# Two layer norms of a convolution mixer moved among other products, and one convolution tile moved from GpSimd to VectorE

## The chip, the cores and the metric

The kernel runs on one core of a Trainium2 chip. The metric is the device time of one execution in microseconds (us). The engines are TensorE (PE: matrix products; PEld: the loads of their weights), VectorE (DVE), ScalarE (ACT), GpSimd (POOL) and SyncE (SP), which issues the transfers. Each engine runs its own instructions strictly in order and waits for the others at semaphores.

## What is computed

Two layers on a sequence of 1024 tokens of width 1024. Layer 0 is a convolution mixer with a layer norm inside, layer 1 a pooling mixer:

```python
def _conv_mixer(h, w_in, dw, db, ln_g, ln_b, w_out):
    a, b, g = jnp.split(h @ w_in, 3, axis=-1)
    y = a * jax.nn.sigmoid(b)
    y = lax.conv_general_dilated(y, dw[:, None, :], ...)  + db     # 31 taps, each channel by itself
    y = jax.nn.silu(_layernorm(y, ln_g, ln_b)) * jax.nn.silu(g)
    return y @ w_out

def _pool_mixer(h, w_in, w_grp, scale, w_out):
    v, g = jnp.split(h @ w_in, 2, axis=-1)
    ...                                                            # window means, products by group
    return (y * jax.nn.silu(g)) @ w_out

for i in range(DEPTH):                                             # per layer
    h = _rms(x, norm_g[i]) * (1.0 + sc) + sh                       # sc, sh, gt from c @ w_mod
    x = x + gt * o
```

## The kernel before

Channels lie on the 128 partitions (8 tiles `ct`), tokens along the row, in two halves `h` of 512. Each float32 operand is split into a high and a low part (`load_split`: ScalarE writes the high part, VectorE or GpSimd the low one), and a product is three matmuls (`mm3`); a whole 1024-deep product (`gemm`) is 24 matmuls into one PSUM bank. The second half's part of layer 0 is worked off beneath the first half's layer 1, since its convolutions run on engines that are free there.

- **Convolutions** (`conv`, `conv_taps`). VectorE does a tile in two PSUM banks of the pool `cv` (tile name `cv`, L482). The tiles in `POOL_CT[h]` go another way: ScalarE multiplies by a tap into `pr` (L469), of which there are two buffers, and GpSimd adds it to `z` (L470). So ScalarE can be at most two taps ahead of GpSimd, and whatever stands behind a tap in ScalarE's order waits too.
- **Gates** (`gate_g`): the products `psg` with weights `wg`; the result goes to DRAM as `sgd` and comes back in `gate_norm`. `CORD` is the order of the tiles: 0, 2, 1, 3, 4, 6, 5, 7. The tiles in `FILL` (4, 6, 5, 7) have their second half done later, beneath another norm.
- **Layer norm** (`layernorm`): TensorE sums over channels (`mr`), ScalarE copies the row, TensorE spreads the mean (`mu`), VectorE subtracts it (L538), ScalarE squares (`sqz`, two buffers), TensorE sums the squares (`vpz`, 128x1 matmuls, L275), then ScalarE, GpSimd (power, `vrz`, L241), ScalarE (`dgz`) and TensorE (`rbz`) make the factor. `gate_norm` then applies factor, silu and gate to each tile and splits it into `y1`, which the output products `pso` need.
- **Layer 1** (`layer1_group`): products `psv` and `psq`, window means on VectorE (`s`), group products `psy`; `layer1_out` does the output products `psf`, four weights at a time first (`wp0` to `wp3`), then one by one.

The order on each engine comes from a scheduler that works by priority from the order of the code; `behind(...)` holds instructions after others, `priority(-LATER)` brings them forward.

Of the kernel before, what the change touches and what calls it, by code (L numbers as in the profile page):

```python
# [12 lines left out]
ALU = mybir.AluOpType  # L13
# [4 lines left out]
KT = 8  # L18
# [3 lines left out]
EPS = 1e-6  # L22
PAD = 8
FIRST = 4
POOL_CT = ((1, 3, 5), (1, 3, 5, 6, 7))
PAIRS = ((0, 2), (1, 3), (4, 6), (5, 7))
CORD = [ct for p in PAIRS for ct in p]
FILL = (4, 6, 5, 7)
# [6 lines left out]
HOLD = (4, 2, 3, 4)  # L35
GAPS = (2, 3, 1, 3)
LAST = 2
SUBS = (2, 4)
MID_OUT = 6
TAIL = 8  # L40
NA = HW - TAIL
# [15 lines left out]
def hybrid_kernel(ctx, tc, xT, vecs, wm, wk, cv_first, cv_w, cv_wo, pl_w, pl_grp, pl_wo, out):  # L57
    nc = tc.nc
# [7 lines left out]
    LATER = 1 << 20  # L66
# [3 lines left out]
    @contextmanager  # L70
    def priority(shift):
        base = tc.cur_priority
        tc.cur_priority = base + shift
        yield
        tc.cur_priority = base

    def step(n=1):
        for _ in range(n):
            if pending and next(pending[0], None) is None:
                pending.pop(0)  # L80

    def unit(tag, name, dt=F32, cols=1024):

        width = WIDTH.get(tag[0], 1024)
        return S.tile([P, width], dt, tag=tag, name=name, bufs=RINGS.get(tag, 1))[:, :cols]
# [4 lines left out]
    def raw(name):  # L90
        return unit("raw", name)

    def bank(tag, name):
        return PS.tile([P, HW], F32, tag=tag, name=name, bufs={"mm": 5, "ax": 1, "cv": 2}[tag])

    def mmps(name):
        return bank("mm", name)
# [4 lines left out]
    def hs(h):  # L102
        return slice(h * HW, (h + 1) * HW)

    def bl(j):
        return slice(j * P, (j + 1) * P)
# [8 lines left out]
    def pair(region, i, name):  # L115
        return unit(f"{region}{i}", name + "h", F32R), unit(f"{region}{i + 1}", name + "l", F32R)
# [48 lines left out]
    def hi_part(hi, src, add=None):  # L165
        if add is None:
            return nc.scalar.copy(hi, src)  # L167
        return nc.scalar.activation(hi, src, AF.Identity, bias=add)
# [15 lines left out]
    @contextmanager  # L184
    def behind(instructions):
        with ExitStack() as stack:
            for i in instructions:
                stack.enter_context(tc.issue_after(i.ins))
            yield
# [5 lines left out]
    def load_split(src, name, slots=None, load=nc.sync.dma_start, eng=nc.vector):  # L195
        r = raw(name)
        load(out=r, in_=src)
        u = pair(*slots, name) if slots else (unit("w", name + "h", F32R), unit("w", name + "l", F32R))
        hi_part(u[0], r)
        lo_part(*u, r, eng=eng)  # L200
        return u
# [24 lines left out]
    power_done, spread_done = [None], [None]  # L226
# [41 lines left out]
    def square_sums(xs, name, vp):  # L268


        def add(i):
            sq = half("sq", f"sq{name}{i}")
            nc.scalar.activation(sq, xs[i], AF.Square)  # L273
            for j in range(4):
                last = nc.tensor.matmul(  # L275
                    vp[:, j : j + 1], sq[:, bl(j)], ones[:, 0:1], start=i + j == 0, stop=i == KT - 1,
                    skip_group_check=True,
                )
            return last

        return (None, vp), add
# [102 lines left out]
    with priority(-LATER):  # L384
        x_done, rb = norm_x(0)
# [59 lines left out]
    def conv(h, ct, taps=None, count=None):  # L445

        with priority(LATER * (1 + h)):
            for _ in islice(taps or conv_taps(h, ct), count):
                pass

    def conv_taps(h, ct):
# [9 lines left out]
        order = [MID, MID - 1] + [k for k in range(TAPS) if k not in (MID, MID - 1)]  # L461
        if ct in POOL_CT[h]:
            for k in order:
# [38 lines left out]

    sgd = [[DR.tile([P, 1024], F32, name=f"sgd{h}{j}") for j in range(4)] for h in range(2)]

    def gate_g(ct, halves, after=(), start=KT // 2):
        wg = load_split(cv_w[2 * KT + ct], f"wg{ct}{halves[0]}")
        for h in halves:
            ps = mmps(f"psg{ct}{h}")
            gemm(ps, wg, hT[h], after, start)
            s = half("sg", f"sgw{ct}{h}")  # L510
            nc.scalar.activation(s, ps, AF.Silu)
            i = CORD.index(ct)
            nc.sync.dma_start(out=sgd[h][i // 2][:, hs(i % 2)], in_=s)

    for i, ct in enumerate(CORD[:6]):
        gate_g(ct, (0,) if ct in FILL else (0, 1))
        step(MODS[1][i])

    sums_done = [None, None]

    def layernorm(h, fill=None, after=None):
        z = [zs[h][ct] for ct in CORD]
        sums = mmps(f"mr{h}")
        row = S.tile([P, HW], F32, tag="row", name=f"mrow{h}", bufs=1)
        mu = axps(f"mu{h}")
        with priority(-LATER):
            for i, ct in enumerate(ZORD[h]):
                g = slice(32 * (i % 4), 32 * (i % 4) + 32)
                nc.tensor.matmul(sums[g, :], onesd[:, :32], zs[h][ct], start=i < 4, stop=i >= 4)
            nc.scalar.copy(row, sums)  # L530
            last = nc.tensor.matmul(mu, selm, row, start=True, stop=True)
        sums_done[h] = last
        if fill is not None:
            fill(GAPS[0], last)
        total, add = square_sums(z, f"z{h}", mmps(f"vpz{h}"))
        for i in range(KT):
            with behind([after[k] for k in range(2) if i >= SUBS[k]] if after else []):
                sub = nc.vector.tensor_tensor(out=z[i], in0=z[i], in1=mu, op=ALU.subtract)  # L538
            with priority(-LATER):
                add(i)  # L540
        if fill is not None:
            fill(GAPS[1], sub)
        return z, *rstd_rows(total, f"z{h}", fill)
# [79 lines left out]
        with behind([ins]):  # L623
            conv(1, 0, early_taps, count)

    z, rb, rb_done = layernorm(0, fill)
    gate_g(CORD[6], (0,), [rb_done], HOLD[0])
    gate_g(CORD[7], (0,), [rb_done], 0)
    y1, done = gate_norm(0, z, rb)
    with behind(done[1:]):  # L630
        conv(1, 0, early_taps)
        for ct in (1, 3):
            conv(1, ct)
        taps = conv_taps(1, 2)
        conv(1, 2, taps, EARLY)
    x1, total = out_half(0, y1, ws, done)
# [8 lines left out]
    h2_0, h2_started, h2_done, rb_done = h2_half(0, x1, total, "Q", 0)  # L645
# [12 lines left out]
    y2, mixed, rest = [[], []], [None, None], []  # L658
# [138 lines left out]
    for g in range(4):  # L797
        group = layer1_group(g, 0, h2_0, early, group if g else None)
        if g == 0:
            with behind([h2_done]):  # L800
                conv(1, 2, taps)
                for ct in range(4, KT):
                    conv(1, ct)
        if g:
            ahead += [load_split(pl_wo[m], f"wp{m}0", ("E", 2 * m)) for m in ((0,), (1,), (2, 3))[g - 1]]
    layer1_out(0, range(MID_OUT - 1), ahead, group)
    with priority(-LATER):
        z, rb, rb_done = layernorm(1, None, mixed)
    with behind(spread_done):
        for finish, m, ps in rest:  # L810
            finish(m, ps)
# [4 lines left out]
    x1, total = out_half(1, y1, ws, done)  # L816
    h2_1, _, _, rb_done = h2_half(1, x1, total, "Y", 2)
# [58 lines left out]
```

## Time and profile before

| | us |
|---|---|
| runs shown (3): median, lowest, highest | 798.62, 798.11, 800.89 |
| profiled execution: its own time | 799.68 |
| span of its instructions | 797.9 |
| busy: PE, DVE, POOL, ACT | 742.0, 555.5, 457.3, 400.9 |

The profiled execution took 799.68 us, of which 797.9 us are the span between its first and its last instruction. Times in the trace count from the start of that span. A busy TensorE is not one at its peak, since its clock has two levels, 1.2 and 2.4 GHz; the granted clock of a stretch is given as a share of the higher one.

### The profile page before, as it was taken

The page shows a single profiled execution, that of the slowest core. Times are in us where ns is not written, and L with a number is a line of the kernel's source. Part 1 is how long each engine was busy: PE and PEld are TensorE (multiplying, and loading weights), DVE is VectorE, ACT ScalarE, POOL GpSimd, SP SyncE. Part 2 cuts the span into 40 slices and gives each one's busy share as a digit, 9 for nine tenths or more (in the row PEclk, how much of TensorE's full clock was granted, in tenths as well). Part 3 has the DMA queues.
Part 4 walks back from the last instruction along what each step waited for, and adds up shares of the span by engine and source line. Part 5 has one row for each costly group of instructions (what it writes and reads, how often), then busy time and mean ns, then how long its engine had stood idle before and what let it go on. Part 6 is the DMA issues. An engine that isn't in the chain of part 4 may idle for free.

```text
span 797.9 us, 9925 instructions
## 1 busy us (share of the span) xinstructions
PE 742.0 (93%) x3564; PEld 590.1 (74%) x3564; DVE 555.5 (70%) x721; ACT 400.9 (50%) x590; POOL 457.3 (57%) x386
## 2 busy tenths in 40 slices
PE   3899999999999968989999879998899889999998
PEld 1777787777776647658877657886788668888998
DVE  6998997928894270899969999973295562566521
ACT  4446466565667677643786665431323432433210
POOL 2001989999988999850999995180112521443322
PEclk7799999999999985999999989999699989999999
DMA  9880013424147550344541124547123630233232
GB/s 328 323 307 25 0 63 123 159 106 153 67 151 300 215 172 1 107 125 152 187 156 53 53 93 131 185 137 257 40 93 119 199 117 1 93 106 132 80 108 81
DMA packets 36481, 105.68 MB, mean 132 GB/s; under 512 B 4048, under 2 KB 6224, under 8 KB 36432
## 3 DMA queue, kind: packets, MB, share of 16 engines
q1 hardware_dynamic: 36432, 105.05, 38.0%
q8 instruction: 28, 0.46, 0.2%
q14 instruction: 21, 0.17, 0.1%
HBM read 92.45 MB, written 12.58 MB: 132 GB/s over the span
## 4 chain that ended last, share of the span: by engine, by line
PE 32%; POOL 30%; DVE 14%; issue 11%; ACT 8%; DMA 3%; SPq 0%; POOLq 0%; ACTq 0%; DVEq 0%
POOL z L470 27%; DVE cv L482 3%; PE psv L206 2%; PE psq L206 2%; PE psq L204 2%; PE psq L205 2%; PE psv L204 2%; PE psv L205 2%; PE psf L204 2%; PE psf L205 2%; PE psf L206 2%; ACT pr L469 2%; PE pso L204 2%; PE pso L205 2%; PE pso L206 2%
## 5 line engine op out<-in xcount | busy, mean ns | idle before, releaser
L470 POOL TENSOR_TENSOR z<-z,pr 128x512 f32<-128x512 f32 (+8 forms) x240 | 348.4, 1452 | 68.0 <-ACT z L466 40.5
L469 ACT ACTIVATE pr<-y,VT 128x512 f32<-128x512 f32 (+8 forms) x240 | 171.0, 719 | 117.6 <-POOL z L470 111.4
L482 DVE SCALAR_TENSOR_TENSOR cv<-y,VT,cv 128x512 f32<-128x512 f32 (+12 forms) x232 | 157.7, 740 | 0.2
L766 DVE SCALAR_TENSOR_TENSOR xf<-psf,gt,xf 128x260 f32<-128x260 f32 (+1 forms) x24 | 13.3, 570 | 38.2 <-PE psf L206 32.1
L241 POOL TENSOR_TENSOR vrx<-vex,mhalf 128x4 f32<-128x4 f32 x2 | 2.0, 1025 | 56.5 <-ACT vex L239 56.5
L560 DVE TENSOR_TENSOR z<-z,rbz 128x512 f32<-128x512 f32 x16 | 10.7, 680 | 32.2 <-PE rbz L247 32.2
L666 DVE TENSOR_TENSOR s<-v 128x519 f32<-128x519 f32 (+1 forms) x16 | 19.4, 1214 | 19.4 <-ACT v L715 19.4
L749 DVE SCALAR_TENSOR_TENSOR q<-psy,VT,q 128x260 f32<-128x260 f32 (+1 forms) x24 | 13.5, 568 | 25.3 <-PE psy L206 25.1
L275 PE MATMUL vpz<-ones,sqz 128*128 128x1 f32 x128 | 22.9, 312 | 8.6 <-ACT sqz L273 8.6
L275 PEld LDWEIGHTS vpz<-ones,sqz 128*128 128x128 f32 x128 | 22.8, 277 | 10.5 <-ACT sqz L273 10.4
L167 ACT CAST y<-q 128x504 fp32r<-128x504 f32 (+1 forms) x16 | 9.9, 618 | 28.7 <-DVE q L749 28.6
L563 ACT ACTIVATE z<-z,VT 128x512 f32<-128x512 f32 x16 | 12.8, 812 | 21.3 <-DVE z L560 21.3
L681 DVE SCALAR_TENSOR_TENSOR s<-s,v 128x504 f32<-128x504 f32 (+1 forms) x16 | 21.0, 1317 | 2.1 <-POOL s L679 2.0
L241 POOL TENSOR_TENSOR vrz<-vez,mhalf 128x4 f32<-128x4 f32 x2 | 2.0, 1019 | 34.9 <-ACT vez L239 34.9
L670 DVE TENSOR_TENSOR s<-s 128x517 f32<-128x517 f32 (+5 forms) x24 | 20.1, 840 | 0.3
L167 ACT CAST pd<-s 128x504 fp32r<-128x504 f32 (+1 forms) x16 | 9.8, 618 | 19.1 <-DVE s L681 14.7
L285 DVE SCALAR_TENSOR_TENSOR wmb<-wmb,s_row 128x1024 f32<-128x1024 f32 x16 | 19.3, 1216 | 0.0
L297 PE MATMUL gv<-wk,srep 128*32 128x256 f32 x256 | 18.6, 386 | 0.2 <-DMA wk<-in_wk 0.2
L172 DVE TENSOR_TENSOR pd<-s,pd 128x504 fp32r<-128x504 f32 (+1 forms) x16 | 16.4, 1034 | 2.9 <-ACT pd L167 2.7
L555 DVE TENSOR_TENSOR z<-z,sgr 128x512 f32<-128x512 f32 x16 | 17.6, 1100 | 1.0 <-ACT z L563 1.0
L577 DVE SCALAR_TENSOR_TENSOR xr<-pso,gt,xr 128x512 f32<-128x512 f32 x16 | 11.7, 746 | 8.1 <-PE pso L206 7.6
L606 DVE SCALAR_TENSOR_TENSOR xr<-xr,a,rby 128x512 f32<-128x512 f32 x16 | 11.6, 736 | 7.9 <-PE rby L247 7.9
(2496 smaller groups left out, 2366.7 us busy)
## 6 DMA issues: line engine op xcount, KB each, us to landing
wk<-in_wk SPq DMA_DIRECT2D x32, 512.0 KB, 5.5
wmb<-in_wm SPq DMA_DIRECT2D x16, 512.0 KB, 6.3
wo<-in_cv_wo SPq DMA_DIRECT2D x16, 512.0 KB, 4.4
wp<-in_pl_wo SPq DMA_DIRECT2D x16, 512.0 KB, 3.3
wg<-in_cv_w SPq DMA_DIRECT2D x12, 512.0 KB, 3.5
wv<-in_pl_w SPq DMA_DIRECT2D x12, 512.0 KB, 3.4
wq<-in_pl_w SPq DMA_DIRECT2D x12, 512.0 KB, 3.4
x<-in_xT SPq DMA_DIRECT2D x16, 256.0 KB, 6.1
```

What stands on the lines that cost most here:

```text
L167: return nc.scalar.copy(hi, src)
L204: nc.tensor.matmul(ps, w[0], r[0], start=first, stop=False)
L205: nc.tensor.matmul(ps, w[0], r[1], start=False, stop=False)
L206: nc.tensor.matmul(ps, w[1], r[0], start=False, stop=last)
L275: last = nc.tensor.matmul(vp[:, j : j + 1], sq[:, bl(j)], ones[:, 0:1], start=i + j == 0, stop=i == KT - 1, skip_group_check=True,)
L285: nc.vector.scalar_tensor_tensor(out=w, in0=w, scalar=1.0, in1=s_row, op0=ALU.mult, op1=ALU.mult, accum_out=out)
L469: nc.scalar.activation(pr[:, o], y[:, i], AF.Copy, scale=dw(k))
L470: nc.gpsimd.tensor_tensor(out=z[:, o], in0=z[:, o], in1=pr[:, o], op=ALU.add)
L482: nc.vector.scalar_tensor_tensor(out=a[:, o], in0=y[:, i], scalar=dw(k), in1=a[:, o], op0=ALU.mult, op1=ALU.add)
L666: nc.vector.tensor_tensor(out=s[:, :m], in0=v[:, :m], in1=v[:, 1 : m + 1], op=ALU.add)
L670: nc.vector.tensor_tensor(out=s[:, :m], in0=s[:, :m], in1=s[:, step : step + m], op=ALU.add)
L681: nc.vector.scalar_tensor_tensor(out=s, in0=s, scalar=1.0 / w, in1=v[:, PAD : PAD + n], op0=ALU.mult, op1=ALU.subtract)
```

## The change

1. `POOL_CT[0]` loses tile 5: its first half is convolved by VectorE, and GpSimd has two tiles of the first half in place of three.
2. The gates' products are done in another order: first tiles 4, 6, 5, 7 for the first half, then 0 and 2 for both, then 1 and 3 for the first half. The second half of 1 and 3, with the weights kept, stands beneath the first layer norm, where the first half of 5 and 7 stood.
3. GpSimd's tile 3 of the second half is held behind the first layer norm (`behind(spread_done)`).
4. The second layer norm is written ahead of the mixer's first output products, its sums go to the two `cv` banks in place of two of the five `mm` banks, and its subtractions no longer wait for the mixer (`mixed`, `SUBS`).

```diff
-POOL_CT = ((1, 3, 5), (1, 3, 5, 6, 7))
+POOL_CT = ((1, 3), (1, 3, 5, 6, 7))
-SUBS = (2, 4)
...
-    def gate_g(ct, halves, after=(), start=KT // 2):
-        wg = load_split(cv_w[2 * KT + ct], f"wg{ct}{halves[0]}")
+    def gate_w(ct, h):
+        return load_split(cv_w[2 * KT + ct], f"wg{ct}{h}")
+
+    def gate_g(ct, halves, after=(), start=KT // 2, wg=None):
+        wg = wg or gate_w(ct, halves[0])
...
-    for i, ct in enumerate(CORD[:6]):
+    for i, ct in enumerate((*FILL, *CORD[:2])):
         gate_g(ct, (0,) if ct in FILL else (0, 1))
         step(MODS[1][i])
+    wg_last = {ct: gate_w(ct, 0) for ct in CORD[2:4]}
+    for ct in CORD[2:4]:
+        gate_g(ct, (0,), wg=wg_last[ct])
...
-    def layernorm(h, fill=None, after=None):
+    def layernorm(h, banks, fill=None):
...
-        sums = mmps(f"mr{h}")
+        sums = bank(banks, f"mr{h}")
...
-        total, add = square_sums(z, f"z{h}", mmps(f"vpz{h}"))
+        total, add = square_sums(z, f"z{h}", bank(banks, f"vpz{h}"))
         for i in range(KT):
-            with behind([after[k] for k in range(2) if i >= SUBS[k]] if after else []):
-                sub = nc.vector.tensor_tensor(out=z[i], in0=z[i], in1=mu, op=ALU.subtract)
+            sub = nc.vector.tensor_tensor(out=z[i], in0=z[i], in1=mu, op=ALU.subtract)
...
-    z, rb, rb_done = layernorm(0, fill)
-    gate_g(CORD[6], (0,), [rb_done], HOLD[0])
-    gate_g(CORD[7], (0,), [rb_done], 0)
+    z, rb, rb_done = layernorm(0, "mm", fill)
+    gate_g(CORD[2], (1,), wg=wg_last[CORD[2]])
+    gate_g(CORD[3], (1,), [rb_done], HOLD[0], wg_last[CORD[3]])
...
-        for ct in (1, 3):
-            conv(1, ct)
+        conv(1, 1)
+        with behind(spread_done):
+            conv(1, 3)
...
+    with priority(-LATER):
+        z, rb, rb_done = layernorm(1, "cv")
     layer1_out(0, range(MID_OUT - 1), ahead, group)
-    with priority(-LATER):
-        z, rb, rb_done = layernorm(1, None, mixed)
```

How this moves instructions is seen on two engines. On ScalarE, at the end of the first layer norm, the squares (`sqz`), the step to the power (`vez`) and the spread factor (`dgz`) stood between taps for GpSimd (`pr`) before:

```order
L273 ACTIVATE sqz_2417<-z_1257 128x512
L469 ACTIVATE pr_3521<-y_1380,VT 128x512
L273 ACTIVATE sqz_2424<-z_1257 128x512
L469 ACTIVATE pr_3524<-y_1380,VT 128x512
L273 ACTIVATE sqz_2431<-z_1437 128x512
L469 ACTIVATE pr_3527<-y_1380,VT 128x512
L273 ACTIVATE sqz_2438<-z_1437 128x512
L469 ACTIVATE pr_3530<-y_1380,VT 128x512
L469 ACTIVATE pr_3533<-y_1380,VT 128x512
L469 ACTIVATE pr_3536<-y_1380,VT 128x512
L239 ACTIVATE vez_2447<-vpz_2387,eps 128x4
```

After the change the same place on ScalarE has no tap in it (line numbers are the changed kernel's own):

```order
L272 ACTIVATE sqz_2374<-z_1257 128x512
L513 ACTIVATE sgw_2444<-psg_2419 128x512
L272 ACTIVATE sqz_2381<-z_1257 128x512
L272 ACTIVATE sqz_2388<-z_1437 128x512
L272 ACTIVATE sqz_2395<-z_1437 128x512
L238 ACTIVATE vez_2404<-vpz_2344,eps 128x4
L245 ACTIVATE dgz_2409<-ident,vrz_2406 128x128 x4
```

What moved: all taps of the stretch. Ahead of `dgz` ScalarE now has 90 taps in place of 161, behind it 120 in place of 79.

On TensorE, at the end of the second layer norm, seven of the eight groups of square sums (`vpz`) stood in one piece behind a part of the last output product (`psf`, weights `wp5`) before:

```order
L205 MATMUL psf_4608<-y_4050,wp50h 128x504
L206 MATMUL psf_4608<-y_4050,wp50l 128x504
L275 MATMUL vpz_4526<-ones,sqz_4535 128x1 x4
L275 MATMUL vpz_4526<-ones,sqz_4542 128x1 x4
L275 MATMUL vpz_4526<-ones,sqz_4549 128x1 x4
L275 MATMUL vpz_4526<-ones,sqz_4556 128x1 x4
L275 MATMUL vpz_4526<-ones,sqz_4563 128x1 x4
L275 MATMUL vpz_4526<-ones,sqz_4570 128x1 x4
L275 MATMUL vpz_4526<-ones,sqz_4577 128x1 x4
L247 MATMUL rbz_4587<-dgz_4588,ones 128x512
L204 MATMUL psf_4608<-y_4061,wp50h 128x504
```

After the change only the last two groups are left there; the six others, `mr` and `mu` stand further up, in pairs among the `psf` products:

```order
L203 MATMUL psf_4553<-y_3995,wp50h 128x504
L204 MATMUL psf_4553<-y_3995,wp50h 128x504
L205 MATMUL psf_4553<-y_3995,wp50l 128x504
L274 MATMUL vpz_4306<-ones,sqz_4350 128x1 x4
L274 MATMUL vpz_4306<-ones,sqz_4357 128x1 x4
L246 MATMUL rbz_4367<-dgz_4368,ones 128x512
L203 MATMUL psf_4553<-y_4006,wp50h 128x504
```

What moved: 15 `psf` matmuls still stand behind `rbz`, but the last two matmuls of `mr` now stand 48 `psf` matmuls behind the first, where all of `mr` stood behind 120 of them.

The third place is ScalarE in the last group of layer 1's first half, where it makes the high parts of the weights `wq5`, `wv6`, `wv7`. Before:

```order
L469 ACTIVATE pr_3778<-y_1800,VT 128x497
L167 CAST wq50h<-wq_4114 128x1024
L715 COPY v_4038<-psv_4013 128x512
L167 CAST grs_4155<-gr_4153 128x512
L167 CAST y_4050<-q_3893 128x504
L167 CAST y_4061<-q_3893 128x504
L167 CAST wv60h<-wv_4159 128x1024
L167 CAST pd_4069<-s_3971 128x504
L735 ACTIVATE q_4080<-psq_4087 128x512
L167 CAST wv70h<-wv_4194 128x1024
```

After the change:

```order
L468 ACTIVATE pr_3651<-y_1745,VT 128x512
L166 CAST wq50h<-wq_4059 128x1024
L720 COPY v_3983<-psv_3958 128x512
L468 ACTIVATE pr_3654<-y_1745,VT 128x512
L166 CAST grs_4100<-gr_4098 128x512
L468 ACTIVATE pr_3657<-y_1745,VT 128x512
L166 CAST y_3995<-q_3838 128x504
L166 CAST y_4006<-q_3838 128x504
L468 ACTIVATE pr_3660<-y_1745,VT 128x512
L468 ACTIVATE pr_3663<-y_1745,VT 128x512
L166 CAST wv60h<-wv_4104 128x1024
```

What moved: before, the tap ahead of `wq50h` was GpSimd's last of the second half. Now taps go on until behind `wo10h`. From `wq40h` on, ScalarE has 21 taps ahead of `wq70h` in place of 2, and 29 ahead of `wo11h` in place of 2; between `vey` (the next norm's step on ScalarE) and `wq40h` there are 45 in both kernels, and between `dgz` and `vey` 46 in place of 32.

## Rows read from the trace of the kernel before

**Rows 1.** Waits of TensorE, longest first: us in total, times, longest.

```profile
PE vpz L275 <- ACT sqz L273: 8.6, 3, 6.4
```

**Rows 2.** Windows: length, busy PE, PEld, DVE, ACT, POOL (instructions), clock, DMA.

```profile
150.00:288.50 138.50, 137.73 (x745) 100.79 (x743) 84.45 (x107) 91.27 (x133) 127.81 (x93) 1.00 0.44 162
288.50:318.65 30.15, 19.87 (x81) 16.92 (x82) 10.79 (x16) 21.88 (x36) 28.48 (x23) 0.65 0.13 44
318.65:354.70 36.05, 30.66 (x113) 22.31 (x113) 32.75 (x35) 21.69 (x31) 28.23 (x19) 0.91 0.29 95
355.00:377.00 22.00, 22.00 (x118) 18.73 (x117) 21.69 (x31) 7.43 (x10) 0.00 (x0) 1.00 0.50 169
449.90:477.20 27.30, 20.50 (x74) 15.25 (x72) 25.95 (x31) 17.60 (x27) 26.71 (x22) 0.87 0.32 106
477.20:522.60 45.40, 44.85 (x193) 35.91 (x192) 43.38 (x57) 22.48 (x31) 18.72 (x19) 1.00 0.43 140
552.90:579.80 26.90, 21.99 (x109) 17.28 (x109) 10.27 (x17) 9.82 (x18) 3.34 (x2) 0.75 0.24 78
```

**Rows 3.** Timeline of TensorE, first layer norm: start, length, instruction, wait ahead.

```profile
288.49 1.10 PE L531 MATMUL mu<-mrow,selm 128*128 128x512 f32 x2 [0.28 <-ACT mrow L530]
...
316.58 2.07 PE L247 MATMUL rbz<-dgz,ones 128*128 128x512 f32 x2 [3.09 <-ACT dgz L246]
...
328.22 0.39 PE L204 MATMUL pso<-y100h,wo00h 128*128 128x512 f32 x1
328.45 0.40 PE L204 MATMUL pso<-y100h,wo01h 128*128 128x512 f32 x1
```

**Rows 4.** Timeline of TensorE in the output products: sixteen square sums.

```profile
361.83 1.84 PE L275 MATMUL vpy<-ones,sqy 128*128 128x1 f32 x16
```

**Rows 5.** Waits of ScalarE in 288.5 to 314.

```profile
ACT pr L469 <- POOL z L470: 5.6, 10, 1.0
```

**Rows 6.** Timeline of VectorE behind the first layer norm.

```profile
324.29 0.94 DVE L556 CAST y100h<-z 128x512 fp32r<-128x512 f32 x1 [1.88 <-PE psg L206]
```

**Rows 7.** Timeline of TensorE, second layer norm.

```profile
552.96 1.92 PE L529 MATMUL mr<-z,onesd 128*32 128x512 f32 x16
...
561.22 9.44 PE L275 MATMUL vpz<-ones,sqz 128*128 128x1 f32 x56
573.42 2.08 PE L247 MATMUL rbz<-dgz,ones 128*128 128x512 f32 x2 [2.76 <-ACT dgz L246]
```

**Rows 8.** Waits of ScalarE in 403 to 487.4.

```profile
ACT pr L469 <- POOL z L470: 20.7, 24, 2.3
```

**Rows 9.** GpSimd's adds by group in 200 to 288: count, busy us, mean ns.

```profile
L470 POOL TENSOR_TENSOR z<-z,pr 128x512 f32<-128x512 f32 (+15 forms) x59 | 82.5, 1399 | 7.9 <-ACT pr L469 4.1
```

**Rows 10.** The same in 449 to 487.5.

```profile
L470 POOL TENSOR_TENSOR z<-z,pr 128x512 f32<-128x512 f32 (+15 forms) x20 | 33.7, 1684 | 1.0
```

**Rows 11.** Timeline of GpSimd: a single add, the slowest run of adds, two splits.

```profile
303.55 1.27 POOL L470 TENSOR_TENSOR z<-z,pr 128x512 f32<-128x512 f32 x1
...
460.04 10.30 POOL L470 TENSOR_TENSOR z<-z,pr 128x510 f32<-128x510 f32 x5
...
518.24 3.24 POOL L172 TENSOR_TENSOR wp40l<-wp,wp40h 128x1024 fp32r<-128x1024 f32 x1 [5.68 <-ACT wp40h L167]
...
525.15 2.41 POOL L172 TENSOR_TENSOR wo11l<-wo,wo11h 128x1024 fp32r<-128x1024 f32 x1
```

**Rows 12.** Timeline of ScalarE, last group of layer 1's first half.

```profile
480.63 1.03 ACT L167 CAST wq40h<-wq 128x1024 fp32r<-128x1024 f32 x1
...
510.19 1.05 ACT L167 CAST wq70h<-wq 128x1024 fp32r<-128x1024 f32 x1 [0.51 <-PE psv L205]
```

**Rows 13.** Timeline of VectorE, then TensorE, there.

```profile
511.28 1.22 DVE L172 TENSOR_TENSOR wq70l<-wq,wq70h 128x1024 fp32r<-128x1024 f32 x1
...
517.10 0.39 PE L204 MATMUL psq<-h200h,wq70h 128*128 128x512 f32 x1
```

**Rows 14.** VectorE's taps in 150 to 288.5: ns lowest, median, highest.

```profile
L482 DVE SCALAR_TENSOR_TENSOR cv<-y,VT,cv x71: 730/741/745, 149.7 to 239.1; 128x512 f32<-128x512 f32 x43, 128x497 f32<-128x497 f32 x2, 128x498 f32<-128x498 f32 x2, 128x499 f32<-128x499 f32 x2
```

## The prediction, on record before the changed kernel ran

> **What bounds the kernel now.** I read the page's busy shares first, where TensorE fills nearly the whole span, so that nothing but its waits and its slow stretches can be won. The list of its waits says where those are: the longest is `vpz` waiting for ScalarE's squares, 8.6 us in all [rows 1]. Then the windows, cut at the places that the diff touches [rows 2]. Five of them matter. From 150 to 288.5 us TensorE never stops and runs at the higher level (1.00), while VectorE is busy for 84.5 of 138.5 us. In the first layer norm (288.5 to 318.65) TensorE is busy for 19.9 of 30.2 us at a clock of 0.65. From there to 354.7 VectorE sets the pace (32.8 of 36.1 us). From 449.9 to 477.2 TensorE stands for 6.8 us and its clock is 0.87, with GpSimd (26.7) and VectorE (26.0 of 27.3) both full; from 477.2 to 522.6 TensorE runs through and GpSimd is less than half busy. The second layer norm (552.9 to 579.8) runs at 0.75. The timelines give the single steps.
>
> Prices at full clock: two output products start 0.23 us apart [rows 3], so a product of 24 costs 5.5 us; sixteen square sums take 1.84 us, 0.115 each [rows 4], so the 64 of one norm cost 7.4 us.
>
> **Gates in another order, and the tile that VectorE takes: +0.5 us.** The tile is some 31 taps of 0.74 us [rows 14], 23 us, and VectorE has 54 us free between 150 and 288.5 [rows 2]. The number of products and loads is the same. What can hurt is that four gates' weights are now needed 5.5 us apart, not 11, while VectorE's order has taps ahead of each low part. Walking VectorE's new order with these durations, the first low part comes at about 216 us, where TensorE needs it, and the next three within 0.5 us of their need. Bounds: nothing, and 3 us, if each of the first four comes 0.75 us late (one tap). I take 0.5, since GpSimd, with 90 taps and not 161 ahead of the norm, is done by about 208 us and no longer works beside these splits.
>
> **First layer norm: -11.2 us.** Before, 29.1 us pass from the end of `mu` (289.59) to the end of `rbz` (318.65) [rows 3]. ScalarE's squares stand between taps, and these waited 5.6 us for GpSimd in that stretch [rows 5]. After the change there is no tap in it, and between `mu` and `rbz` TensorE has 36 gate products (8.3 us) and 64 square sums (7.4), then the wait for the power and the spread, 3.1 [rows 3], and `rbz`, an estimated 1.0 at full clock (half of its 2.07): 19.8 us, so 9.3 less. Then `y100h` waited 1.9 us for the last first-half gate product, since `y1` overwrites that half's input [rows 6]; the products left in this place now are of the second half, so this goes too. What is late next is VectorE's own chain to 354.7 us, of unchanged length, so that all 11.2 us pass on. TensorE's clock does not matter in that chain. Bounds: 1.9, if the 15.7 us of products take twice as long at the lower level as they do at the higher, and 13, if VectorE's chain, which shares its time with GpSimd, shortens a little too.
>
> **Second layer norm: -4.5 us.** From 552.9 to 579.8 TensorE had 24 output products (5.5), `mr` (1.9), `mu` (1.0), square sums (7.4) and `rbz` (1.0): 16.8 us of work in 26.9. Now `mr`, `mu` and six of the eight groups of square sums stand among 120 products that run without a gap. What stays is the end: two groups of sums, a wait of 2.8 us [rows 7], and the slow `rbz` and products behind it, 1.1 + 1.8 us over their full-clock time: 5.7 of the 10.1 us lost. Bounds: -7.3 (the clock stays up) and -2.
>
> **GpSimd's backlog: +4.2 us, and +2.9 us behind it.** This is what the change pays. Holding a tile behind the first norm leaves 120 adds behind it in place of 79. Fourteen of the 41 more stand ahead of the next norm, where GpSimd did nothing at all from 355 to 377 us [rows 2]: 14 x 1.4 [rows 9] is 20 us, which hides them, and the work that VectorE has there is mostly taps of one SBUF operand. Between that norm and `wq40h` nothing is added (45 taps in both). The other 27 come between `wq40h` and `wo11h`, where GpSimd was free, and ScalarE's weight casts now queue behind them, as its taps in 403 to 487 queued behind GpSimd for 20.7 us [rows 8]. Up to `wq70h` there are 21 adds: at 1.68 us each, their mean in 449 to 487 [rows 10], with 3 us of small copies, 38.4 us, where `wq40h` to `wq70h` took 29.6 [rows 12]. So that cast comes 8.8 us late; its low part used to be ready 4.6 us early (512.50 against 517.10) [rows 13], which leaves 4.2. Bounds: at 1.40 us per add it is 2.8 us late and hidden, nothing; at the slowest run, 2.06 us [rows 11], it is 16.7 late, 12.1 us.
>
> Then `z` of tile 7 is done later. Behind `wq70h` (now ending at 520.0) come eight more adds (13.5) and three weight splits of 2.4 us [rows 11], which stand between them in GpSimd's order: 540.7. TensorE comes to the last two matmuls of `mr` 48 products into `psf`: 522.6 + 4.2 + 11.1 = 537.9. So it waits 2.9 us. Bounds: 0 at 1.40 us per add, and 8.3 at 2.06, if each of the three splits also takes the 3.24 us that the longest took [rows 11].
>
> Here a rule of the Trainium skill speaks against the change. An add alone took 1.27 us, and five in a row beside VectorE's work 10.30, 2.06 each [rows 11]. The Trainium skill's page SBUF — State Buffer, section Who interferes with whom, says that a VectorE instruction with two SBUF inputs and a GpSimd instruction that reads SBUF exclude each other, each for the other's whole length. By it, an add that meets one split of 1.22 us [rows 13] would take 2.49 us, and with all 21 adds so the backlog would be 21 us in place of 4.2. The trace's slowest run lies between the two, its mean nearer to the single add.
>
> **Sum:** 0.5 - 11.2 - 4.5 + 4.2 + 2.9 = -8.1 us against the profiled execution's 799.7 us: 791.6. The median of the runs shown is 1.1 us under that execution, so 790.5. About 0.5%, 4 us, is what a measurement of this kernel can tell from no change: 794.6 and 802.6 are the borders.
>
> **Rivals.**
> - *The adds fit in* (16%). GpSimd keeps the 1.40 us that it had beside VectorE's taps. For it: in 477 to 522 VectorE's work is in part such taps. Against it: the rest is window sums and weight splits. Then neither 4.2 nor 2.9 is paid: 784.5 by the profile, 783.4 by the median.
> - *The backlog takes more than the norms give* (14%, slower). The place is 477 to 530 us: adds and VectorE's two-operand work shut each other out, ScalarE's casts `wv60h` to `wq70h` wait behind taps, TensorE waits for weights, and then for `mr`. For it: 449.9 to 477.2, where all three engines are as full as they will be here, lost 6.8 us of TensorE's time in 27. Against it: VectorE's part there is no larger than before. At 2.06 us and with the long splits: 0.5 - 11.2 - 4.5 + 12.1 + 8.3 = +5.2, 803.8 by the median. It decides from 1.83 us per add on, where the two terms pass 11.2 us and the gain falls below 0.5%; at 1.97 nothing is left of it, and slower by over 0.5% takes the slowest rate with the long splits. The rule of the Trainium skill's page SBUF — State Buffer, section Who interferes with whom, makes this the likelier case; the mean of 1.68 here does not bear it out.
> - *The first norm gives only half* (15%). The squares no longer wait for GpSimd, but the products among the sums hold them back in their turn, or the clock falls again in a stretch with much waiting: 5.6 us less gain, -2.5, 796.1 by the median. For it: the clock was 0.65 there. Against it: TensorE now has products to do between the sums.
>
> **How the numbers follow.** The forecast has 55%, and with its bounds halved gives 786 to 795.5. Faster by over 0.5%: 50 of these 55, and the 16 of the first rival: 66%. Within: 5 and 13 of the third: 18%. Slower: 14, and 2 of the third with the backlog at its upper end: 16%. The range reaches from the first rival's 783.4, and a little below it, over the third, to a few us short of the second's 803.8: 782 to 800.5.
>
> **What would show it.** Right: `rbz` of the first norm ends about 20 us behind `mu`, with no tap among the squares, and the granted clock there is near 1.00; `y100h` waits for no gate product; no gap longer than 3 us from `psf` to `pso` in the second half; GpSimd busy nearly all the time from 477 to about 530 us (less the shift), adds of about 1.7 us, and TensorE's waits there for `wv6`, `wv7`, `wq6` or `wq7`. Wrong: a clock of 0.65 still in the first norm; a wait of over 5 us ahead of `mr` in the second; gates' products waiting for low parts of `wg` at 216 to 245 us.

## The result, and the profile after

The changed kernel took 805.55 us (median of 4 runs, 805.08 to 806.57) against 798.41 of the kernel before beside it: ratio 1.0084, 95% interval 1.0062 to 1.0107. It is slower by 0.8%, where 790.5 was forecast. The profiled execution's span grew by 6.9 us, from 797.9 to 804.8.

I cut both spans at the same instructions of TensorE: first `mu`, first `pso`, first `vpy`, `rby` of the first half, first `psq` with `wq70`, first `pso` of the second half. The last column is the forecast of the same stage.

| stage, us | before | after | change | forecast |
|---|---|---|---|---|
| start to `mu` | 288.49 | 286.14 | -2.35 | +0.5 |
| `mu` to `pso` (first norm) | 39.73 | 31.02 | -8.71 | -11.2 |
| `pso` to `vpy` (VectorE's chain) | 33.61 | 38.71 | +5.10 | 0 |
| `vpy` to `rby` | 43.03 | 42.37 | -0.66 | 0 |
| `rby` to `wq70` (layer 1, first half) | 112.24 | 128.90 | +16.66 | +4.2 |
| `wq70` to `pso` (second norm) | 62.72 | 62.28 | -0.44 | -4.5 + 2.9 |
| to the end | 218.08 | 215.38 | -2.70 | 0 |

At the first `pso` the changed kernel is 11.1 us ahead, near the 10.7 of the forecast, but by luck: the first row gave 2.9 us more than forecast and the second 2.5 less. It loses all of that, and more, in two stages. The four middle stages as windows of the kernel before, with the columns of [rows 2] (length, then busy PE, PEld, DVE, ACT, POOL, clock, DMA):

```profile
288.49:328.22 39.73, 29.45 (x116) 24.61 (x117) 17.74 (x23) 28.04 (x45) 37.32 (x29) 0.70 0.12 40
328.22:361.83 33.61, 28.22 (x109) 20.44 (x108) 32.92 (x39) 17.85 (x26) 19.40 (x12) 0.95 0.47 155
404.86:517.10 112.24, 104.17 (x425) 80.48 (x423) 106.81 (x131) 68.84 (x103) 83.71 (x74) 0.97 0.32 106
517.10:579.82 62.72, 57.81 (x265) 46.41 (x264) 30.52 (x33) 19.23 (x30) 21.23 (x12) 0.89 0.42 138
```

The same of the changed kernel, with the stretch ahead of its first norm as the first row:

```profile
208.00:286.00 78.00, 78.00 (x445) 55.35 (x444) 43.94 (x63) 22.83 (x31) 2.35 (x2) 1.00 0.59 206
...
286.14:317.16 31.02, 25.80 (x119) 20.63 (x117) 14.06 (x20) 13.62 (x24) 6.72 (x6) 0.78 0.10 34
317.16:355.87 38.71, 29.52 (x108) 20.13 (x109) 38.23 (x42) 21.03 (x30) 28.13 (x19) 0.96 0.41 136
...
398.24:527.14 128.90, 110.46 (x442) 83.85 (x442) 122.61 (x127) 83.31 (x125) 116.24 (x96) 0.93 0.28 91
527.14:589.42 62.28, 54.99 (x253) 44.05 (x252) 34.71 (x38) 24.12 (x38) 31.08 (x19) 0.95 0.44 151
```

Read VectorE's column (the third busy time) and its instruction counts. In layer 1's first half it has four instructions fewer (127 in place of 131), yet is busy for 122.6 us in place of 106.8: 15.8 us more, about what the stage lost. In the chain it is full in both kernels (32.9 of 33.6, 38.2 of 38.7), and longer by 5.3. GpSimd did 2.35 us of work in the 78 us ahead of the norm, where its adds alone took 82.5 us from 200 to 288 before [rows 9]; that work now stands in the two stages that lost. The groups show where VectorE's time went (count, busy us, mean ns), first of the kernel before from 404.86 to 517.10, then of the changed one from 398.24 to 527.14:

```profile
L666 DVE TENSOR_TENSOR s<-v 128x519 f32<-128x519 f32 x8 | 7.1, 892 | 0.0
...
L172 DVE TENSOR_TENSOR pd<-s,pd 128x504 fp32r<-128x504 f32 x6 | 4.5, 743 | 0.0
...
L172 DVE TENSOR_TENSOR y<-q,y 128x504 fp32r<-128x504 f32 x5 | 3.5, 720 | 0.1
...
L470 POOL TENSOR_TENSOR z<-z,pr 128x512 f32<-128x512 f32 (+15 forms) x46 | 73.4, 1597 | 3.4 <-ACT pr L469 1.0
```

```profile
L481 DVE SCALAR_TENSOR_TENSOR cv<-y,VT,cv 128x512 f32<-128x512 f32 (+15 forms) x52 | 36.5, 739 | 0.0
L671 DVE TENSOR_TENSOR s<-v 128x519 f32<-128x519 f32 x8 | 9.5, 1186 | 0.0
...
L171 DVE TENSOR_TENSOR pd<-s,pd 128x504 fp32r<-128x504 f32 x6 | 6.3, 1045 | 0.0
L171 DVE TENSOR_TENSOR y<-q,y 128x504 fp32r<-128x504 f32 x4 | 6.1, 1517 | 0.0
...
L469 POOL TENSOR_TENSOR z<-z,pr 128x512 f32<-128x512 f32 (+7 forms) x68 | 105.4, 1551 | 9.5 <-ACT pr L468 6.6
```

GpSimd has 68 adds there in place of 46, each no slower (1.55 against 1.60 us). VectorE pays: what reads two SBUF operands grew (`y` from 0.72 to 1.52 us), while taps, with one, kept their 0.74. TensorE's waits of the changed kernel, 398 to 535 us, name VectorE's late weight splits (the parts with `l`):

```profile
PE psv L205 <- DVE wv40l L171: 7.0, 1, 7.0
PE psq L205 <- DVE wq30l L171: 3.4, 1, 3.4
PE psv L205 <- DVE wv60l L171: 3.0, 1, 3.0
```

ScalarE did not make these splits late. The cast of `wv40h` had ended at 464.73, and VectorE, with no idle time from 456 to 471 us, came to the split 5.5 us later (start, length); the casts for `wq30l` and `wv60l` had ended 2.8 and 2.2 us ahead of their splits:

```profile
463.68 1.05 ACT L166 CAST wv40h<-wv 128x1024 fp32r<-128x1024 f32 x1
...
464.89 1.74 DVE L171 TENSOR_TENSOR y<-q,y 128x504 fp32r<-128x504 f32 x1
...
470.23 2.26 DVE L171 TENSOR_TENSOR wv40l<-wv,wv40h 128x1024 fp32r<-128x1024 f32 x1
```

The loss does not begin with the later adds, which stand behind ScalarE's cast `wq40h`. The stage cut at that cast, first before, then after:

```profile
404.86:480.63 75.77, 68.25 (x271) 51.90 (x270) 71.41 (x82) 51.56 (x79) 72.62 (x61) 0.95 0.23 76
480.63:517.10 36.47, 35.92 (x155) 28.59 (x153) 35.40 (x49) 17.28 (x25) 11.08 (x14) 1.00 0.51 168
```

```profile
398.24:480.40 82.16, 66.74 (x261) 50.13 (x262) 76.34 (x83) 53.37 (x82) 70.67 (x62) 0.94 0.23 76
480.40:527.14 46.74, 43.72 (x182) 33.72 (x180) 46.27 (x45) 29.95 (x44) 45.57 (x35) 0.93 0.37 119
```

Ahead of the cast 6.4 us are lost, with 44 adds in place of 43, in the mean no slower (1.46 against 1.56 us; the add that crosses the cut counts on both sides), and VectorE is busy for 4.9 us more; the two longest waits above, for `wv40l` and `wq30l`, stand there. Behind it 10.3 us are lost, with 25 adds in place of 4 and VectorE full throughout; 27 more matmuls of TensorE stand there too.

The second norm on TensorE: the last matmuls of `mr` wait for GpSimd's last tile, 16 us behind the first `psf` (532.68), and `mu` comes 24 us behind it, so the square sums no longer hide among the products ([rows 7] has the steps of before):

```profile
548.67 1.05 PE L534 MATMUL mr<-z,onesd 128*32 128x512 f32 x4 [3.77 <-POOL z L469]
556.35 1.02 PE L536 MATMUL mu<-mrow,selm 128*128 128x512 f32 x2
...
583.46 1.30 PE L246 MATMUL rbz<-dgz,ones 128*128 128x512 f32 x2 [2.76 <-ACT dgz L245]
```

### The profile page after: what moved, and what is told of

Read it like the earlier page. It is cut to its first block, busy times and chain, and to the rows that moved or that the text cites. A ratio compares the mean times of both kernels' runs of the same rounds, so it can differ in the third digit from the quotient of the medians.

```text
span 804.8 us, 9866 instructions
## 1 busy us (share of the span) xinstructions
PE 736.9 (92%) x3564; PEld 582.9 (72%) x3564; DVE 588.6 (73%) x754; ACT 380.4 (47%) x560; POOL 421.4 (52%) x356
## 4 chain that ended last, share of the span: by engine, by line
PE 56%; POOL 17%; DVE 11%; issue 7%; ACT 4%; DMA 4%; SPq 0%; POOLq 0%; ACTq 0%; DVEq 0%
POOL z L469 13%; PE ps L203 4%; PE ps L205 4%; PE ps L204 4%; PE psg L203 3%; PE psg L205 3%; PE psg L204 3%; PE psf L203 2%; PE pso L204 2%; PE psf L204 2%; PE psf L205 2%; PE pso L205 2%; PE pso L203 2%; PE psq L205 2%; PE gv L296 2%
## 5 line engine op out<-in xcount | busy, mean ns | idle before, releaser
L469 POOL TENSOR_TENSOR z<-z,pr 128x512 f32<-128x512 f32 (+8 forms) x210 | 311.5, 1484 | 49.6 <-ACT pr L468 21.9
L468 ACT ACTIVATE pr<-y,VT 128x512 f32<-128x512 f32 (+8 forms) x210 | 149.7, 719 | 101.4 <-POOL z L469 97.2
L481 DVE SCALAR_TENSOR_TENSOR cv<-y,VT,cv 128x512 f32<-128x512 f32 (+15 forms) x261 | 177.5, 742 | 0.2
L671 DVE TENSOR_TENSOR s<-v 128x519 f32<-128x519 f32 (+1 forms) x16 | 21.8, 1362 | 19.4 <-ACT v L720 19.4
L754 DVE SCALAR_TENSOR_TENSOR q<-psy,VT,q 128x260 f32<-128x260 f32 (+1 forms) x24 | 13.4, 569 | 26.3 <-PE psy L205 26.2
L564 DVE TENSOR_TENSOR z<-z,rbz 128x512 f32<-128x512 f32 x16 | 10.7, 680 | 20.6 <-PE rbz L246 20.6
L675 DVE TENSOR_TENSOR s<-s 128x517 f32<-128x517 f32 (+5 forms) x24 | 23.1, 965 | 0.2
L272 ACT ACTIVATE sqz<-z 128x512 f32<-128x512 f32 x16 | 10.0, 631 | 23.9 <-PE vpz L274 18.8
L171 DVE TENSOR_TENSOR y<-q,y 128x504 fp32r<-128x504 f32 (+1 forms) x16 | 17.4, 1090 | 3.7 <-ACT y L166 3.7
L274 PEld LDWEIGHTS vpz<-ones,sqz 128*128 128x128 f32 x128 | 16.6, 204 | 2.4 <-ACT sqz L272 1.8
L513 ACT ACTIVATE sgw<-psg 128x512 f32<-128x512 f32 x16 | 9.5, 592 | 18.5 <-issue 11.1
L559 DVE TENSOR_TENSOR z<-z,sgr 128x512 f32<-128x512 f32 x16 | 17.3, 1080 | 1.0 <-ACT z L567 1.0
```

What stands on the lines that cost most here:

```text
L171: return eng.tensor_tensor(out=lo, in0=src, in1=hi.bitcast(F32), op=ALU.subtract)
L468: nc.scalar.activation(pr[:, o], y[:, i], AF.Copy, scale=dw(k))
L469: nc.gpsimd.tensor_tensor(out=z[:, o], in0=z[:, o], in1=pr[:, o], op=ALU.add)
L481: nc.vector.scalar_tensor_tensor(out=a[:, o], in0=y[:, i], scalar=dw(k), in1=a[:, o], op0=ALU.mult, op1=ALU.add)
L671: nc.vector.tensor_tensor(out=s[:, :m], in0=v[:, :m], in1=v[:, 1 : m + 1], op=ALU.add)
L675: nc.vector.tensor_tensor(out=s[:, :m], in0=s[:, :m], in1=s[:, step : step + m], op=ALU.add)
```

## The experiments

Theory: the hold empties GpSimd ahead of the first norm and puts its adds beside VectorE's two-operand work, which they lengthen. Rivals: the second norm's new place costs the time; the tile that VectorE took, or the gates' order, does; ScalarE's weight casts queue behind taps that wait for GpSimd. Ratios are to the kernel before in the same runs (801.1 to 802.8 us there).

**E1: the hold undone.**

```diff
-        with behind(spread_done):
-            conv(1, 3)
+        conv(1, 3)
```

> The changed kernel without its part 3: tile 3 of the second half is no longer held behind the first norm, so 152 of the 210 adds stand ahead of the first norm's factor, not 90, and 2 and not 29 behind the cast of wq40. Theory (the 27 late adds lengthen VectorE's two-operand instructions from 400 to 532 us and so delay its weight splits): the first norm loses its new gain again (its squares stand between taps), some 4 to 7 us, but the first psf comes at 518 to 523 us and not at 532.7, with no wait of TensorE over 3 us for wv40 or wv60: 794 to 798 us. Rival (the second norm's new place costs the time): still over 803.

Measured: 780.37 us, ratio 0.9716 (0.9689 to 0.9744), so adding the hold to the other three parts turns a gain of 2.8% into a loss, and the second norm's place is not the cost. The first `psf` came at 515.23. The time is still 14 us below what I expected, because two stages gave more than I knew:

```profile
289.05:324.69 35.64, 27.30 (x116) 22.35 (x117) 12.98 (x21) 15.78 (x27) 12.33 (x11) 0.71 0.09 30
324.69:350.35 25.66, 25.66 (x109) 19.52 (x108) 25.18 (x41) 9.59 (x12) 0.00 (x0) 1.00 0.63 207
393.42:508.49 115.07, 106.09 (x438) 80.57 (x438) 108.89 (x134) 69.60 (x103) 85.42 (x75) 0.97 0.31 104
508.49:559.79 51.30, 51.30 (x251) 41.79 (x250) 25.96 (x34) 19.58 (x30) 19.12 (x12) 1.00 0.49 159
```

With GpSimd at rest beside VectorE's chain (second row, POOL 0.00) it takes 25.7 us, not 33.6 or 38.7. And with `z` in time the second norm hides whole: TensorE is busy for all of 51.3 us, where before it took 62.7.

**E2: the hold one tile later.** Tile 3 runs free; the tiles behind it are held.

```diff
-        with behind(spread_done):
-            conv(1, 3)
+        conv(1, 3)
...
-                for ct in range(4, KT):
-                    conv(1, ct)
+                with behind([spread_z]):
+                    for ct in range(4, KT):
+                        conv(1, ct)
```

> The changed kernel with the hold one tile later: tile 3 of the second half runs freely ahead of the first norm (GpSimd stood idle there from 208 to 308 us), and only tiles 5, 6 and 7 are held behind the norm; 120 adds stand ahead of the factor and none among the squares. Theory: it keeps the first norm's lead of 6.6 us and has the kernel before's backlog from 400 us on, so psf at about 516 us and 788 to 794 us in all. Rival (second norm's place): over 799. Rival (the tile that VectorE took, or the gates' order, costs it later): 797 to 803.

Measured: 783.56 us, ratio 0.9763 (0.9737 to 0.9789), below the interval expected by one of E1's two stages, the second norm (51.3 us again from `wq70` to `pso`). Thirty adds moved into GpSimd's idle stretch are worth 3.2 points against the changed kernel. The stage from `rby` to `wq70` is 115.08 us, the chain still 38.85 with 20 GpSimd instructions beside it:

```profile
316.54:355.39 38.85, 29.61 (x108) 20.41 (x109) 38.37 (x42) 22.08 (x32) 30.25 (x20) 0.96 0.42 137
398.19:513.27 115.08, 106.70 (x439) 81.14 (x438) 108.95 (x134) 69.55 (x103) 85.48 (x75) 0.97 0.31 103
```

**E3: the gates' order and the second norm's place alone**, on the kernel before (parts 2 and 4 of the diff; tile 5 stays on GpSimd, nothing is held).

> The kernel before with parts 2 and 4 alone: the gates' order and the second norm's place, with tile 5 still on GpSimd and no hold. Theory: 240 adds and the same backlog as before, so no loss from 400 to 523 us; the second norm gives some 1 to 3 us, the gates' order about none: 795 to 799. Rival (the second norm's place costs): 801 or more.

Measured: 792.09 us, ratio 0.9867 (0.9843 to 0.9890), better than expected. From `wq70` to `pso` it takes 51.30 us against 62.72, and from `rby` to `wq70` 2.1 us more, since 14 of the 16 matmuls of `mr` now stand there and not behind it; net, the new place gives 9.3 us. The chain from `pso` to `vpy` took 35.96 us, 2.4 more than before:

```profile
406.62:520.95 114.33, 106.58 (x439) 81.08 (x437) 108.92 (x134) 68.80 (x103) 84.72 (x75) 0.97 0.31 104
520.95:572.25 51.30, 51.30 (x252) 41.80 (x250) 25.92 (x34) 19.69 (x30) 19.15 (x12) 1.00 0.48 159
```

**E4: the changed kernel with the old second norm** (part 4 undone).

> The changed kernel without its part 4: the second norm stands again behind the mixer's first output products, in the mm banks, with its subtractions held as before. Theory (backlog): psf still at about 532 us; what the second norm's new place gave is lost: 805.5 to 810. Rival (the second norm's new place costs the time): 796 to 801.

Measured: 814.48 us, above the interval expected; ratio 1.0153 (1.0126 to 1.0181), 0.7 points over the changed kernel's 1.0084: even here the new place is worth 5.6 us from `wq70` to `pso`, of which 2.0 are paid ahead of `wq70`, so that rival falls. The old norm takes 67.8 us here against 62.7 before; the late adds are not shown as the cause, since the profiled execution of E8, which holds none, took 67.4:

```profile
524.74:592.58 67.84, 60.14 (x265) 47.30 (x264) 36.93 (x40) 24.13 (x38) 33.67 (x21) 0.87 0.42 143
```

**E5: held until the chain's end.** As E2, but tiles 5, 6 and 7 wait for the last silu of the first norm's gates.

```diff
+    norm_end = done[0]
...
-                with behind([spread_z]):
-                    for ct in range(4, KT):
+                conv(1, 4)
+                with behind([norm_end]):
+                    for ct in (5, 6, 7):
                         conv(1, ct)
```

> Like e2, but tiles 5, 6 and 7 are held until the last silu of the first norm's gates and not only until its factor is spread. In e2 VectorE's chain from the first pso to the first vpy took 38.9 us with GpSimd's released adds beside it, in e1 25.7 us with GpSimd idle there. Theory (adds and VectorE's two-operand instructions shut each other out in that chain): it falls to 26 to 31 us, the later backlog grows by some ten adds and takes back up to 5: 773 to 781 us. Rival (the chain's length has another cause, such as the order of VectorE's taps in it): 782 to 788.

Measured: 782.88 us, ratio 0.9783 (0.9746 to 0.9820), no better than E2. The time lies in the rival's interval, but not for its reason: the chain fell as expected, even to 23.83 us, but the adds kept out of it came back later and cost as much: `rby` to `wq70` 123.78 us, 8.7 over E2, and `vpy` to `rby` 48.98 in place of 42.80:

```profile
316.65:340.48 23.83, 23.83 (x99) 17.76 (x98) 23.32 (x38) 13.47 (x19) 7.19 (x5) 1.00 0.64 207
389.46:513.24 123.78, 110.82 (x441) 83.12 (x440) 117.74 (x136) 77.44 (x116) 104.25 (x87) 0.94 0.29 97
```

**E6: a partial hold.** As E5, and the first 21 taps of tile 5 ahead of the norm.

```diff
+        taps5 = conv_taps(1, 5)
+        conv(1, 5, taps5, 21)
...
-                    for ct in (5, 6, 7):
+                    conv(1, 5, taps5)
+                    for ct in (6, 7):
                         conv(1, ct)
```

> Like e5, but the first 21 taps of tile 5 run ahead of the first norm as well, so that GpSimd is busy up to the norm (140 adds ahead of it), does nothing beside it and beside the chain behind it, and has the backlog of e1 after it (45 adds behind the next norm's spread). Theory: the norm as short as in the changed kernel (mu to pso 31 us against 35.6 in e1), the chain as in e1 (26 to 28 us): 772 to 779 us, the fastest of all. Rival (what is kept away there comes back from 400 us on): 780 or more, as e1.

Measured: 772.70 us, ratio 0.9650 (0.9615 to 0.9685), as expected, and the fastest kernel that does all the work. GpSimd works up to the norm and rests in it (1.02 us in the second row), the chain stays short, and layer 1 has the backlog of E1:

```profile
208.00:286.00 78.00, 76.42 (x435) 53.20 (x434) 52.02 (x62) 53.68 (x79) 73.23 (x51) 1.00 0.56 202
...
288.20:316.65 28.45, 24.48 (x119) 19.70 (x118) 13.02 (x21) 9.16 (x17) 1.02 (x1) 0.82 0.10 38
316.65:343.31 26.66, 26.56 (x111) 19.82 (x110) 26.18 (x38) 15.47 (x22) 11.28 (x8) 1.00 0.57 185
386.21:501.36 115.15, 106.80 (x438) 81.14 (x438) 108.95 (x134) 69.61 (x103) 85.50 (x75) 0.97 0.31 103
```

**E7: GpSimd busy without reading SBUF.** This separates the theory from ScalarE's queue.

```diff
-                    nc.gpsimd.tensor_tensor(out=z[:, o], in0=z[:, o], in1=pr[:, o], op=ALU.add)
+                    if h == 1 and ct != 1:
+                        for _ in range(3):
+                            nc.gpsimd.memset(pr[:, o], 0.0)
+                    else:
+                        nc.gpsimd.tensor_tensor(out=z[:, o], in0=z[:, o], in1=pr[:, o], op=ALU.add)
```

> The changed kernel with the adds of GpSimd's held tiles (3, 5, 6 and 7 of the second half) replaced by three memsets of the same tap buffer each, so these tiles stay unconvolved: ScalarE still waits for GpSimd at each tap, and GpSimd stays about as busy, but it reads no SBUF. Theory (two-operand instructions of VectorE and GpSimd's reads exclude each other): from 405 to 530 us VectorE's weight splits take 1.2 and not 2.2 us, TensorE's waits for wv40, wq30 and wv60 go, and from the second rby of the first half to wq70 it takes 112 to 118 us in place of 128.9. Rival (ScalarE's casts queue behind taps that wait for GpSimd): the splits may be short, but the waits stay and that stretch takes 124 to 131 us. The time as a whole also loses the wait for z, so it is read from that stretch: theory 780 to 793, rival 796 or more.

Measured: 761.16 us, ratio 0.9505 (0.9469 to 0.9540); the stage from `rby` to `wq70` 102.91 us, below both ranges. Its window, groups in it, and ScalarE's wait in 380 to 486:

```profile
382.51:485.42 102.91, 102.91 (x448) 81.17 (x447) 95.43 (x136) 76.45 (x116) 93.31 (x202) 1.00 0.34 115
```

```profile
L675 DVE TENSOR_TENSOR s<-v 128x519 f32<-128x519 f32 x8 | 5.5, 691 | 0.0
...
L171 DVE TENSOR_TENSOR y<-q,y 128x504 fp32r<-128x504 f32 x6 | 4.0, 676 | 0.6 <-ACT y L166 0.6
...
L471 POOL MEMSET pr<- 128x512 f32 (+15 forms) x173 | 85.5, 523 | 7.4 <-ACT pr L468 4.2
```

```profile
ACT pr L468 <- POOL pr L471: 17.3, 20, 2.8
```

Three memsets take 1.57 us, as long as an add took; GpSimd is busy for 93 of 103 us, and ScalarE still waits 17.3 us for it (20.7 before [rows 8], 32.1 in this stage of the changed kernel). Yet `y` takes 0.68 us, and TensorE has no wait left in the stage. So what lengthens VectorE's instructions is not that GpSimd is busy, but its SBUF reads. Since ScalarE's waits halved too, this run alone does not rule out its queue; that rests on the three splits above, which waited for VectorE with their casts done. Fewer taps stand in the stage here (173 memsets are 58 of them, against 68 adds), so the 26 us to the changed kernel are not the reads' alone; VectorE's mean times are.

**E8: VectorE takes the tile, alone**, on the kernel before.

```diff
-POOL_CT = ((1, 3, 5), (1, 3, 5, 6, 7))
+POOL_CT = ((1, 3), (1, 3, 5, 6, 7))
```

> The kernel before with part 1 alone: VectorE takes tile 5 of the first half, nothing is held. Theory: the 30 adds fewer leave GpSimd with 11 adds in place of 32 between the two norms of the first half, so the chain from pso to vpy falls from 33.6 to some 26 us: 2.4 to 1.2 per cent are not expected of the gates, but 8 to 12 us of this, 788 to 795 us against 798 to 803 of before. Rival (VectorE's 31 more taps cost as much as GpSimd's adds gave): 797 to 803.

Measured: 787.60 us, ratio 0.9826 (0.9781 to 0.9871), just below the lower edge. The tile is a gain, and where expected: from `pso` to `vpy` 24.79 us, with GpSimd at rest there. The profiled execution was the longest of the four (794.30 us), and part of its gain went again in the second norm, as E4 says.

**E9: eighteen of VectorE's taps ahead of the norm as well**, on E6.

```diff
+    conv(1, 0, early_taps, 18)
     z, rb, rb_done = layernorm(0, "mm", fill)
```

> Like e6, and VectorE does 18 taps of tile 0 of the second half ahead of the first norm, where it stood idle for some 15 of 25 us from 250 to 275 us, so that 13 us of taps less stand behind the norm. Theory (VectorE is the bound from the first pso to the first half's psf, and GpSimd's adds lengthen its two-operand work there): 4 to 10 us less than e6, 763 to 769 us. Rival (the stretch behind the norm is bounded by the adds alone, or the idle VectorE is held by another wait): 771 to 776.

Measured: 781.82 us, ratio 0.9763 (0.9731 to 0.9795), so worse than E6. The time lies outside both intervals. The chain is as long as in E6 (26.60 us), and VectorE merely idles from 350 to 375 us, where it had been full (first E6, then E9):

```profile
350.00:375.00 25.00, 25.00 (x124) 20.96 (x124) 25.00 (x31) 15.66 (x21) 15.15 (x9) 1.00 0.48 158
...
350.00:375.00 25.00, 25.00 (x122) 20.57 (x121) 16.58 (x14) 18.37 (x27) 23.67 (x16) 1.00 0.42 142
```

And from `rby` to `wq70` it takes 122.31 us (115.15 in E6) with fewer adds, 39 against 46, while VectorE's two-operand instructions got longer (`y` 0.98 us against 0.71). Why fewer adds hurt more stays open, as in the changed kernel ahead of `wq40h`: the order of the instructions on the engines changed too, and no run parts it from the number of adds.

## Why the prediction was wrong, step by step

**The step that failed is GpSimd's backlog (+4.2 us).** The stage lost 16.7. The forecast priced the 21 later adds ahead of `wq70h` by GpSimd's pace and followed the delay along ScalarE's casts. The pace held (1.55 us measured, 1.68 taken), and so did ScalarE's delay: `wq40h` to `wq70h` took 40.2 us (480.40 to 520.62), 38.4 were forecast. But TensorE did not wait for that cast; it waited for VectorE's splits, 13.4 us in the three waits shown. VectorE has its two-operand instructions lengthened, and it was full: [rows 2] gave 43.4 of 45.4 us from 477.2 to 522.6, and of that I drew no conclusion. Its 15.8 us are about the stage's 16.7. In E1 and E2, without the full hold, 13.8 of these are gone, and E3 puts most of the rest, 2.1, down to the place of `mr`; in E7, with GpSimd busy but reading no SBUF, the stage is 9.3 us shorter than before. "VectorE's part there is no larger than before", my ground against the second rival, was the mistake: it had no more instructions, and they got longer. That rival gave 803.8, near the result, but by adds of 2.06 us, which never came.

**"Between that norm and `wq40h` nothing is added" failed too.** Its ground was the number of taps, which did stay the same, but 6.4 of the 16.7 us were lost there, with VectorE busy for 4.9 us more. So the number of adds does not set the price alone. In E1, E2, E3 and E6, with 43 adds there, `rby` to `wq40h` took 75.8 to 76.6 us, against 82.2 with the 44 of the changed kernel. The likely reason, which no run shows by itself, is which of VectorE's instructions the adds meet.

Of the signs that I had named for being wrong none came: the clock in the first norm was 0.78, `mr` of the second waited 3.77 us, and no gate product waited for `wg`. They looked at the norms and the gates, and none at VectorE.

The rule of the Trainium skill's page SBUF — State Buffer, section Who interferes with whom, applies here on VectorE's side: a VectorE instruction with two SBUF inputs contends with a GpSimd instruction that reads SBUF, not with one that only writes it. The trace agrees on both: 1.52 us for `y` beside adds, 0.68 beside memsets. I had weighed the rule only as a price on the add.

**"All 11.2 us pass on" failed** for the same reason. VectorE's chain was taken as of unchanged length; GpSimd's released adds stand beside it and made it 5.1 us longer. E1 and E8, where GpSimd rests there, show 25.7 and 24.8, and E5, with 7.2 us of GpSimd's work, 23.8.

**The first norm (-11.2) was right in kind and too large**: -8.7. From the end of `mu` to the end of `rbz` it gave 4.5 of the 9.3 us, and from there to `pso` 4.2 where 1.9 were forecast. No tap stands among the squares now, but they wait for TensorE in their turn, which has gate products between the sums, and the granted clock was 0.78, not 1.00; both are the third rival's mechanism. The term's lower bound did not follow from its own sum: with 15.7 us of products taking twice as long, the 19.8 us become 35.5, which is a loss of 4.5 in all and not a gain of 1.9. The waits of ScalarE from 288 to 310 us show the first part:

```profile
ACT sqz L272 <- PE vpz L274: 9.1, 5, 5.3
```

E2 and E6 show that a norm as short (29.2 and 28.5 us, with 5.6 and 1.0 us of GpSimd's work in it) needs GpSimd quiet only in it, not empty ahead of it.

**The second norm (-4.5) and the wait behind it (+2.9) were both far too small**; that they nearly cancel, as forecast, is luck. With `z` in time the stage gives 11.4 us (E3: 51.30 against 62.72), 9.3 net of what `mr` takes ahead of it; in the changed kernel 0.4. The wait of `mr` itself is 3.77 us, about the forecast, but its lateness undoes the hiding of most of what stands behind it. Priced on its own as a wait, a late `mr` looked cheap.

**The gates and the tile (+0.5) came out as forecast**, by the runs that do not hold: `mu` came at 289.05, 289.02 and 288.88 in E1, E3 and E8, 0.4 to 0.6 us later than before. The 2.35 us by which it came earlier in the changed kernel are the hold's (286.35 in E4, which holds the same). What the term left out is what the tile gives behind the norm: E8 shows 1.7% for it alone. Whether the gates' order costs something there, as E3's longer chain may say, no run parts. The last stage's -2.7 us was not foreseen, and its cause stays open: in E1 to E6 and in E8 this stage took 218.1 to 218.8 us.

## What to carry to other kernels

When work moves on GpSimd, price it by what VectorE does beside it: count VectorE's instructions with two SBUF operands there, look up their durations beside adds and alone in the same trace, and ask whether VectorE has room. The number of adds is not enough for a price: about the same number cost 6.4 us more in the changed kernel, and 39 cost more in E9 than 46 in E6. Hold an engine back only over the stretch that it disturbs: the full hold cost 3.7 points against no hold (ratios 1.0084 and 0.9716), while one that lets it work up to the norm gained 0.7 more (0.9650). And a wait at the head of a chain placed to be hidden costs the hiding, not its own length.

## What was not expected of the hardware

A cast of one SBUF operand is lengthened too, as these two of VectorE's chain in the changed kernel show, both `y102h`, beside adds and in a gap of them:

```profile
330.51 1.37 DVE L560 CAST y102h<-z 128x512 fp32r<-128x512 f32 x1
...
335.31 0.43 DVE L560 CAST y102h<-z 128x512 fp32r<-128x512 f32 x1
```

The memsets of E7 lengthened casts as well, though not the two-operand instructions: of the eight casts of that chain five took 0.67 to 0.78 us and three 0.43. The Trainium skill's page SBUF — State Buffer, section Who interferes with whom, says that casts too can take the ports that VectorE shares with GpSimd. These rows agree, but which port held a cast up no run here shows.
